# Four feature chunks of a residual turned to token rows by DMA transposes of 16-bit halves instead of TensorE transposes

## The chip, the cores and the metric

The kernel runs on one core of a Trainium2 chip. The metric is device time in microseconds of one execution, taken as the median of the runs. Engine names are those of the profile: PE is TensorE's matmul, PEld its weight load, DVE is VectorE, ACT is ScalarE, POOL is GpSimd, SP is SyncE, which issues most loads.

## The reference

One layer of a streaming encoder on 512 tokens of 1024 features, all in 32-bit floats:

```python
hn = rmsnorm(h, norm_mix_g)
proj = hn @ w_in                       # queries, keys, values, gates of two mixers
h = h + concat(forgetting_attention(...), hgrn2_recurrence(...)) @ w_out
h = h + cross_attention(rmsnorm(h, norm_x_g), rmsnorm(mem, norm_mem_g), w_xq, w_xkv, w_xo)
u = rmsnorm(h, norm_ff_g) @ w1         # 1024 -> 4096
h = h + square(relu(u)) @ w2           # 4096 -> 1024
return rmsnorm(h, final_norm_g)
```

## The kernel before

Every matrix product is made of three matmuls of numbers split in a high part (`wh...`, rounded by a ScalarE copy, line 207) and a low part (`wl...`, the rest, by a VectorE subtraction, line 212). The MLP's products follow Strassen's scheme: a group of 512 hidden units has seven block products, named 1 to 7, and weights of some of them are sums of blocks.

The change lies in the stage between cross attention and MLP. There `residual` (line 1419) makes `h + o @ w_xo` with the features on the partitions: eight chunks `c` of 128 features by 512 tokens, each a product `xw` of 24 matmuls into a bank of its own (`mm`, three banks). The weights of two neighbouring chunks form a panel (38 to 41, halves a and b). When chunk c's product is done, VectorE adds it into `hTc(c)` (`hT`, line 1450), ScalarE writes the high part of the scaled chunk (`x`, line 1452) and VectorE the low part (line 1453). Then `hooks[c]`, here `at4`, `at5` and `at6` (lines 2228 to 2249), prepare the MLP's first group: splits of its first weights, sums of its blocks (`wr`, line 1829), scaled copies of `hT` (line 1974) and their differences `xd` (line 1989), from which the operands `xs` of products 5, 6, 7 and 3 are made (lines 2003 to 2016).

The last products of the kernel want the residual with tokens on the partitions: `acc[tb]`, four tiles of 128 tokens by 1024 features. So each chunk is also turned: `tok_T` (line 1668) makes four TensorE transposes of 128x128 into a PSUM bank `ht`, `tok_copy` copies them to `acc`, half on ScalarE and half on VectorE (lines 1678 and 1680). `residual` calls this for two chunks at a time, after chunks 2, 4 and 6; chunks 6 and 7 follow inside the first group of the MLP (line 2290). `acc` is first read in the MLP's second group.

Loads stand on SP's queue, which issues them in order; each waits for the buffer it writes. The blocks of the first group are `wru01`, `wru02`, `wru05` and `wru06`: the loads of line 1810 for products 1 and 2 and for the sums. Work on each engine stands in an order that the scheduler sets from priorities; from chunk 7 on (line 2258) the order of ScalarE and VectorE is written out by hand. `behind(at, first, why)` (line 189) orders one instruction after another on its engine. `t2` tiles are 2 KB for each partition, ten buffers.

Of the kernel before, what the change touches and what calls it, by code (L numbers as in the profile page):

```python
# [9 lines left out]
F32 = mybir.dt.float32  # L10
R = mybir.dt.float32r
U8 = mybir.dt.uint8
AF = mybir.ActivationFunctionType
ALU = mybir.AluOpType
AX = mybir.AxisListType

P = 128
S = 512
NT = S // P
# [17 lines left out]
FX = (4.4, 4.4, 5.4, 5.4), (3.3, 3.9, 4.5, 5.1)  # L37
X1, X2, X3, X4 = 1.5, 2.0, 1.5, 2.0
NEG = -3.0e38
SEVEN = (1, 2, 3, 4, 5, 6, 7)  # L40
RAWS, HB, LOADS = 5, 4, 8
COPIES = {12: 2, 19: 1, 20: 0, 24: 1}
# [4 lines left out]
def emit(  # L47
# [21 lines left out]
    nc = tc.nc  # L69
    te, ve, ac, gp = nc.tensor, nc.vector, nc.scalar, nc.gpsimd  # L70
# [38 lines left out]
    def t2(name, dt=F32, shape=(S,)):  # L109
        return t2p.tile([P] + list(shape), dt, tag="t2", name=name)  # L110

    def sm(n, name):
        if n > 8:
            return s3p.tile([P, n], F32, tag="s3", name=name, padded_shape=[P, 32])
        return smp.tile([P, n], F32, tag="sm", name=name, padded_shape=[P, 8])
# [13 lines left out]
    def f(a):  # L129
        return a.bitcast(F32)  # L130
# [58 lines left out]
    def behind(at, first, why):  # L189
        tc.add_manual_dep(at.ins, first.ins.name, order_only, reason=why)  # L190
# [7 lines left out]
    def split_made(name, what, at):  # L198
        at_split[name, what] = at
        if (name, what) in pinned:  # L200
            behind(at, pinned[name, what], "split later")

    def split_of(hi, lo, raw, name=None):
        def split(what="hl"):
            at = None
            if "h" in what:
                at = ac.activation(hi, raw, AF.Copy)  # L207
                split_made(name, "h", at)
# [37 lines left out]
    def load_next(parts=(1, 1), between=None):  # L246

        i = len(stream)
        if i >= len(specs):
            return []  # L250
        if callable(specs[i]):
            return specs[i]()
        units, splits = [], []
        uk = specs[i][0][1].shape[1] // 2
        for n in range(2):
            note = None if between is None else (lambda q, at=sum(parts[:n]): between(at + q))
            unit, some = load_unit(f"{i}{'ab'[n]}", specs[i], slice(n * uk, (n + 1) * uk), parts[n], note)
            units.append(unit)
            splits += some
        stream.append(tuple([u[x] for u in units] for x in range(2)))  # L260
        return splits
# [211 lines left out]
    act0 = sm(1, "act0")  # L473
    ac.activation(act0, zero[:, 0:1], AF.Identity)
    first = load_next((4, 2), more_x)
# [24 lines left out]
    def norm_rows(t, name):  # L500
        ms = sm(2, name + "m")
        for i in range(2):
            junk = t2(f"{name}j{i}")
            ac.activation(junk, t[:, i * S : (i + 1) * S], AF.Square, scale=1.0 / 32.0, accum_out=ms[:, i : i + 1])
        ve.tensor_tensor(ms[:, 0:1], ms[:, 0:1], ms[:, 1:2], ALU.add)
# [5 lines left out]

    mku = cp.tile([P, 2, 6, 32], U8, name="mku")
    for half in range(2):
# [41 lines left out]
    def sum_jobs(kind, g):  # L555
        block = {"u": block1, "d": block2, "q": block_q}[kind]
        shape = [P, 2, S] if kind == "d" else [P, UK, WT]
        for name in SUMS:
            wsum[kind, g, name] = drp.tile(shape, F32, name=f"ws{kind}{g}{name}")

        def first(name):
            dma = nc.sync.dma_start(wsum[kind, g, name], block(g, SUMS[name][0]))
            copied.add((kind, g, name))
            return dma

        def sums():
            for name, (_, b) in SUMS.items():
                while (kind, g, name) not in copied:
                    copies.popleft()()
                src = wsum[kind, g, b] if b in SUMS else block(g, b)  # L570
                more = {"max_dma_last_dim": 2048} if b in SUMS else {}
                yield gp.dma_start(wsum[kind, g, name], src, accum_op=ALU.add, **more)  # L572

        return [lambda name=name: first(name) for name in SUMS], sums()
# [32 lines left out]
    for g in range(DFF // HG):  # L607
        if g + 1 in SEVEN:
            sets.append(sum_jobs("u", g + 1))
# [19 lines left out]
    def x_hi(c):  # L629
        ac.activation(hn_hi[:, c, :], xps[c], AF.Identity, scale=g_mix[:, c : c + 1])  # L630

# [3 lines left out]
    def x_park(c):  # L635
        part, dst = c // 2, park[:, c, :]
        if c % 2 == 0:
            ac.activation(dst, xps[c], AF.Copy)
        else:
# [5 lines left out]
    def x_sq(tb):  # L645
        junk = s4([D], f"x0j{tb}")
        if tb < 3:
            ac.activation(junk, xt[:, tb, :], AF.Square, scale=1.0 / 32.0, accum_out=ms0[:, tb : tb + 1])
        else:
# [5 lines left out]
    with tc.manual_schedule(engines={mybir.EngineType.Activation, mybir.EngineType.DVE}):  # L655
# [56 lines left out]
        for c in range(KC):  # L712
            if c in (1, 2):
                rows_of(c, wt0[0], hn_hi)
                rows_of(c, wt0[1], hn_hi)
                at = rows_of(c, wt0[0], hn_lo)
# [46 lines left out]
        def qt_(h):  # L763
            return (Mv, Sa)[h % 2][h // 2][:, h % 2, :]
# [58 lines left out]
    for hp in range(2):  # L823
# [8 lines left out]
        for j in range(2):  # L832
# [4 lines left out]
            at = ac.activation(qt_(h), qt_(h), AF.Silu)  # L837
# [111 lines left out]
    for hp in range(2):  # L949
        Ac.append(t2(f"Ac{hp}", F32, (8, 64)))  # L950
        at = ve.tensor_tensor(Ac[hp], dgs[hp], id64.unsqueeze(1).to_broadcast([P, 8, 64]), ALU.mult)
        for j in range(2):
            h = 2 * hp + j
            at = ve.tensor_tensor(qt_(h), qt_(h), Fg[hp][:, j, :], ALU.mult)
# [52 lines left out]
    for li, m in enumerate(mlev):  # L1007
# [8 lines left out]
        for hp in range(2):  # L1016
            M_ = Mv[hp]
            mix = mixed[hp]
            w = 64 if m == 64 else 32
# [8 lines left out]
        for hp, ps in enumerate(lvs):  # L1028
# [8 lines left out]
            else:  # L1037
                A_ = s4([8, P], f"A{hp}")
                Ag.append(A_)
                lo_, hi_ = slice(0, 64), slice(64, P)  # L1040
# [129 lines left out]
    for c in range(NT):  # L1170
# [27 lines left out]
        with ahead(P1):  # L1198
            hs = sm(4, f"hs{c}")
            for h in range(4):  # L1200
                j = t2(f"hj{c}{h}", F32, (P,))
                at = ac.activation(j, po[:, h, :], AF.Square, scale=128.0 ** -0.5, accum_out=hs[:, h : h + 1])
# [72 lines left out]
    def fox_bias(u):  # L1275
# [5 lines left out]
        gp.tensor_scalar(bi[:, 0:n], fF[h][:, 0:n], -1.0, Ft[:, tb, h : h + 1], op0=ALU.mult, op1=ALU.add)  # L1281
        gp.affine_select(out=bi[:, ts_], in_=bi[:, ts_], compare_op=ALU.is_ge, fill=NEG, base=0, pattern=[[-1, P]], channel_multiplier=1)

# [10 lines left out]
    def fox_softmax(u, ps):  # L1294
        p, tb, j = u
        h, n = 2 * p + j, (tb + 1) * P
        with ahead(P3):

            b = prob[u][:, 0:n]
            mx = sm(1, f"mx{h}{tb}")  # L1300
            ve.tensor_tensor_reduce(out=b, in0=ps[:, 0:n], in1=b, scale=-1.0, scalar=-NEG, op0=ALU.add, op1=ALU.min, accum_out=mx)  # L1301
            den = sm(1, f"dn{h}{tb}")
# [66 lines left out]
    for n in range(len(pairs) + 2):  # L1369
        if n < len(pairs):  # L1370
            p, tb = pairs[n]
# [41 lines left out]
    def hTc(c):  # L1413
        return hT[c // 2][:, c % 2, :]

    run_now(fill_rest(fill))
    load_hT()

    def residual(src_hi, src_lo, g, dst, name, ssq, order, nlast, after=None, hooks={}, open_end=False):

        ps_, gens = {}, {}

        def open_(c):
            if c % 2 == 0:
                open_.wt = next_panel()
            ps_[c] = mm(f"{name}{c}")
            gens[c] = gemm_fm(ps_[c], open_.wt, (c % 2) * P, src_hi, src_lo, order=order, late=True)

        def early():

            for ks in (range(UK), range(UK, KC - nlast)):
                for c in range(3):
                    if c not in gens:
                        open_(c)
                    for _ in ks:
                        yield next(gens[c])

        def rest():
            for _ in range(nlast if gens else 0):
                for gen in list(gens.values()):  # L1440
                    yield next(gen)
            for c in range(KC):
                if c not in gens:
                    open_(c)
                yield from gens[c]
                if open_end and c == KC - 1:
                    last_xw.append(ps_[c])
                    return
                hc = hTc(c)
                ve.tensor_tensor(hc, hc, ps_[c], ALU.add)  # L1450
                hi_, lo_, src = dst(c, hc)
                ac.activation(hi_, src, AF.Identity, scale=g[:, c : c + 1])
                ve.scalar_tensor_tensor(lo_, src, g[:, c : c + 1], f(hi_), op0=ALU.mult, op1=ALU.subtract)
                if ssq is None:
                    pass
                elif c == 0:
                    ac.activation(ssq, hc, AF.Square)
                else:
                    sq = t2(f"{name}sq{c}")
                    ac.activation(sq, hc, AF.Square)  # L1460
                    gp.tensor_tensor(ssq, ssq, sq, op=ALU.add)
                if after is not None and c in (2, 4, 6):
                    after(c - 2)
                    after(c - 1)
                hooks.get(c, lambda: None)()

        return early, rest
# [194 lines left out]

    acc = []

    def to_tok(c):
        tok_copy(c, tok_T(c))

    def tok_T(c):
        ps = tr(f"ht{c}")
        for tb in range(NT):  # L1670
            te.transpose(ps[:, tb * P : (tb + 1) * P], hTc(c)[:, tb * P : (tb + 1) * P], ident)
        return ps

    def tok_copy(c, ps):
        for tb in range(NT):
            d, s_ = acc[tb][:, c * P : (c + 1) * P], ps[:, tb * P : (tb + 1) * P]
            if tb % 2 == 0 or c > 5:
                ac.activation(d, s_, AF.Copy)
            else:
                ve.tensor_copy(d, s_)  # L1680
# [577 lines left out]
    with tc.manual_schedule(engines={mybir.EngineType.Activation, mybir.EngineType.DVE}):  # L2258
        c = KC - 1
# [109 lines left out]
```

## Time and profile before

| | |
|---|---|
| median of 3 runs | 737.67 us (737.52 to 737.95) |
| the profiled execution | 737.33 us, span 735.6 us |
| PE busy | 728.3 us, 99% |
| DVE busy | 596.8 us, 81% |
| ACT busy | 489.2 us, 67% |
| POOL busy | 177.5 us, 24% |
| DMA | 163.89 MB, 223 GB/s in the mean |
| granted TensorE clock | 0.999 |

A row of the timeline gives start and duration in us, engine, line, operation, output and input, and in brackets the idle time of the engine before it and who ended it. A row of the chain gives start, duration, engine, name and line. The profile names tiles without their numbers: `wru` is any of the blocks above, `ht` any of the transposed chunks. A shape is partitions by elements.

The stage in stretches that begin and end at chunk borders of TensorE's stream, with the busy time of each engine (count of instructions in brackets):

```profile
389.30:395.60 6.30, 6.30 (x33) 5.37 (x32) 6.22 (x11) 5.39 (x11) 0.82 (x2) 1.00 0.81 164
395.60:401.10 5.50, 5.50 (x25) 4.48 (x25) 2.90 (x6) 1.67 (x2) 1.53 (x2) 1.00 1.06 273
401.10:407.40 6.30, 6.30 (x33) 5.38 (x32) 4.16 (x8) 3.78 (x8) 1.56 (x2) 1.00 0.93 184
407.40:412.90 5.50, 5.50 (x26) 4.48 (x25) 4.83 (x5) 1.67 (x2) 0.94 (x1) 1.00 0.62 98
412.90:419.20 6.30, 6.30 (x33) 5.36 (x32) 5.25 (x10) 4.25 (x9) 1.12 (x2) 1.00 0.77 94
```

The columns are the stretch and its length, then PE, PEld, DVE, ACT and POOL busy, the granted clock, the mean busy share of the DMA engines, and GB/s.

### The profile page before, as it was taken

To read this page: it belongs to the slowest core of one execution; us is meant where nothing else is said; L and a number is where in the kernel's file an instruction comes from. 1 tells how busy PE (TensorE), PEld (TensorE's weight loads), DVE (VectorE), ACT (ScalarE), POOL (GpSimd) and SP (SyncE) were. 2 spreads that over 40 slices of the span, in tenths; PEclk is the share of its full clock that TensorE was granted. 3 is DMA by queue.
4 is the path that set the end of the run, shared out by engine and by line. 5 is a ranking of instruction groups with operands and counts; after the bars stand their busy time and mean duration, and the time that the engine had idled before them with its cause. 6 is when DMAs were issued, how large, how long until landed. Compare 5 with 4: busy or idle time off the path is not lost.

```text
span 735.6 us, 11788 instructions
## 1 busy us (share of the span) xinstructions
PE 728.3 (99%) x4227; PEld 625.1 (85%) x4227; DVE 596.8 (81%) x1006; ACT 489.2 (67%) x850; POOL 177.5 (24%) x253
## 2 busy tenths in 40 slices
PE   9999999999999999999999999999999999999996
PEld 6789888998888888889988898888888888888885
DVE  6868997777877846767747898998989898989896
ACT  5967776566666644547535589777676767684964
POOL 7122101443432415422111202111111111100024
PEclk9999999999999999999999999999999999999999
DMA  7789969847946999987868799989998899978352
GB/s 244 240 235 257 329 217 294 279 172 239 340 165 195 289 297 267 226 186 145 210 130 185 119 243 230 248 233 258 211 263 210 242 243 229 249 190 249 121 115 114
DMA packets 115819, 163.89 MB, mean 223 GB/s; under 512 B 6529, under 2 KB 77482, under 8 KB 115762
## 3 DMA queue, kind: packets, MB, share of 16 engines
q1 hardware_dynamic: 87538, 117.24, 47.6%
q0 software_dynamic: 28064, 45.64, 34.8%
q8 instruction: 33, 0.54, 0.3%
q10 hardware_dynamic: 160, 0.27, 0.1%
q14 instruction: 24, 0.20, 0.1%
HBM read 157.87 MB, written 54.54 MB: 289 GB/s over the span
## 4 chain that ended last, share of the span: by engine, by line
PE 97%; issue 1%; DMA 1%; DVE 0%; ACT 0%; POOL 0%; POOLq 0%; DVEq 0%
PE uU L1939 11%; PE uY L1939 5%; PE U L2097 4%; PE U L2098 4%; PE U L2099 4%; PE uV L1939 3%; PE xk L1260 2%; PE wo L373 2%; PE xw L373 2%; PE xw L374 2%; PE xw L375 2%; PE wo L375 2%; PE wo L374 2%; PE Y L2099 2%; PE Y L2098 2%; PE Y L2097 2%
## 5 line engine op out<-in xcount | busy, mean ns | idle before, releaser
L207 ACT ACTIVATE whu<-wru 128x1024 fp32r<-128x1024 f32 x53 | 55.1, 1059 | 36.6 <-PE U L2099 17.7
L212 DVE TENSOR_TENSOR wlu<-wru,whu 128x1024 fp32r<-128x1024 f32 x53 | 64.1, 1220 | 12.0 <-ACT whu L207 12.0
L212 DVE TENSOR_TENSOR wld<-wrd,whd 128x1024 fp32r<-128x1024 f32 x56 | 67.9, 1216 | 1.7 <-ACT whd L207 1.7
L207 ACT ACTIVATE whd<-wrd 128x1024 fp32r<-128x1024 f32 x56 | 59.3, 1060 | 10.5 <-PE uU L1939 2.9
L2097 PE MATMUL U<-whd,hb 128*128 128x512 f32 x120 | 46.8, 390 | 0.0
L2098 PE MATMUL U<-wld,hb 128*128 128x512 f32 x120 | 46.8, 390 | 0.0
L2099 PE MATMUL U<-whd,hb 128*128 128x512 f32 x120 | 46.7, 389 | 0.0
L1281 POOL TENSOR_SCALAR bi<-nF,Ft 128x128 f32<-128x128 f32 (+3 forms) x32 | 20.2, 639 | 53.1 <-PE pt L1326 37.0
L572 POOL DMA_DIRECT2D wsd<-in_w_dram x16 | 17.5, 1094 | 59.1 <-PE xw L375 13.7
L1786 POOL DMA_DIRECT2D wrd<-in_w_dram x8 | 9.8, 1222 | 88.1 <-DVE wld L212 76.9
L1786 POOL DMA_DIRECT2D wru<-in_w_dram x7 | 9.2, 1315 | 79.6 <-DVE wlu L212 79.6
L1939 PE MATMUL uY<-xs,whu 128*128 128x512 f32 x112 | 28.0, 392 | 0.0
L1939 PE MATMUL uU<-x,whu 128*128 128x512 f32 x112 | 27.7, 389 | 0.0
L1939 PE MATMUL uU<-xs,whu 128*128 128x512 f32 x112 | 27.7, 389 | 0.0
L2064 DVE SCALAR_TENSOR_TENSOR acc<-Y,acc 128x512 f32<-128x512 f32 x28 | 19.0, 685 | 10.2 <-PE Y L2099 9.8
L2099 PEld LDWEIGHTS U<-whd,hb 128*128 128x128 f32 x120 | 22.5, 188 | 4.7
L2097 PEld LDWEIGHTS U<-whd,hb 128*128 128x128 f32 x120 | 22.6, 188 | 4.5
L2098 PEld LDWEIGHTS U<-wld,hb 128*128 128x128 f32 x120 | 22.6, 188 | 4.4
L572 POOL DMA_DIRECT2D wsu<-in_w_dram x14 | 17.8, 1271 | 34.8 <-PE xw L375 17.7
L1303 ACT ACTIVATE bi<-bi,mx 128x128 f32<-128x128 f32 (+3 forms) x32 | 17.9, 560 | 11.2 <-DVE mx L1301 10.0
L2097 PE MATMUL Y<-whd,hb 128*128 128x512 f32 x64 | 24.9, 389 | 0.0
L2098 PE MATMUL Y<-wld,hb 128*128 128x512 f32 x64 | 24.9, 389 | 0.0
(1061 smaller groups left out, 2546.9 us busy)
## 6 DMA issues: line engine op xcount, KB each, us to landing
wru<-in_w_dram SPq DMA_DIRECT2D x25, 512.0 KB, 6.9
wsd<-in_w_dram SPq DMA_DIRECT2D x24, 512.0 KB, 7.5
wrd<-in_w_dram SPq DMA_DIRECT2D x24, 512.0 KB, 7.0
wrd<-wsd SPq DMA_DIRECT2D x24, 512.0 KB, 6.0
wsu<-in_w_dram SPq DMA_DIRECT2D x21, 512.0 KB, 8.6
wru<-wsu SPq DMA_DIRECT2D x21, 512.0 KB, 5.8
wsd<-in_w_dram POOLq DMA_DIRECT2D x16, 512.0 KB, 8.2
wsu<-in_w_dram POOLq DMA_DIRECT2D x14, 512.0 KB, 9.2
```

The source lines that it names most:

```text
L207: at = ac.activation(hi, raw, AF.Copy)
L212: at_lo = ve.tensor_tensor(lo, raw, f(hi), ALU.subtract)
L373: te.matmul(ps, wh, hi, start=n_ == 0 and not begun, stop=False)
L374: te.matmul(ps, wb, lo, start=False, stop=False)
L375: at = te.matmul(ps, wc, hc, start=False, stop=k == order[-1])
L572: yield gp.dma_start(wsum[kind, g, name], src, accum_op=ALU.add, **more)
L1281: gp.tensor_scalar(bi[:, 0:n], fF[h][:, 0:n], -1.0, Ft[:, tb, h : h + 1], op0=ALU.mult, op1=ALU.add)
L1786: tc.keep_in_program_order(gp.dma_start(box[0], block(g, "10"), accum_op=ALU.add))
L1939: at = te.matmul(out_, w[:, k, ws], x_[:, k, :], start=begin, stop=end, skip_group_check=True)
L2097: te.matmul(ps, hi, whi[:, k, :], start=begin, stop=False, skip_group_check=True)
L2098: te.matmul(ps, hi, wlo[:, k, :], start=False, stop=False, skip_group_check=True)
L2099: at = te.matmul(ps, lo, whi[:, k, :], start=False, stop=k == 1, skip_group_check=True)
```

## The change

Chunks 0 to 3 leave TensorE. A chunk's 32-bit words are seen as pairs of 16-bit halves. ScalarE copies the chunk apart, first all lower halves and then all upper ones (`hw`, 128 x 2 x 512). A DMA on SP's queue that transposes 16-bit elements turns the eight blocks of 128x128 halves into `tw` (token on the partition; half, token block, feature along the row). Copies on ScalarE and VectorE then put the halves together again as 32-bit words in `acc`. Chunks 0 and 1 are put into `acc` after chunk 5, chunks 2 and 3 after chunk 6; chunks 4 and 5 keep the TensorE transposes and also follow after chunk 6. Chunks 6 and 7 are as before.

```diff
+U16 = mybir.dt.uint16
+XB = 4
+AT = {5: (0, 1), 6: (2, 3, 4, 5)}
...
                 hi_, lo_, src = dst(c, hc)
-                ac.activation(hi_, src, AF.Identity, scale=g[:, c : c + 1])
-                ve.scalar_tensor_tensor(lo_, src, g[:, c : c + 1], f(hi_), op0=ALU.mult, op1=ALU.subtract)
+                at_parts[:] = (
+                    ac.activation(hi_, src, AF.Identity, scale=g[:, c : c + 1]),
+                    ve.scalar_tensor_tensor(lo_, src, g[:, c : c + 1], f(hi_), op0=ALU.mult, op1=ALU.subtract),
+                )
...
-                if after is not None and c in (2, 4, 6):
-                    after(c - 2)
-                    after(c - 1)
+                if after is not None:
+                    to_halves(c)
+                    for c_ in AT.get(c, ()):
+                        after(c_)
                 hooks.get(c, lambda: None)()
...
+    halves = {}
+
+    def words(ap):
+        return ap.bitcast(U16).rearrange("p (n w) -> p w n", w=2)
+
+    def to_halves(c):
+        if c < XB:
+            own, turned = t2(f"hw{c}", U16, (2, S)), t2(f"tw{c}", U16, (2, NT, P))
+            ac.activation(own, words(hTc(c)), AF.Copy)
+            nc.sync.dma_start(turned.rearrange("p w t n -> p (w t) n"), own.rearrange("p w n -> p (w n)"), transpose=True)
+            halves[c] = turned
+
     def to_tok(c):
-        tok_copy(c, tok_T(c))
+        if c not in halves:
+            return tok_copy(c, tok_T(c))
+        turned = halves.pop(c)
+        for tb in range(NT):
+            d, s_ = words(acc[tb][:, c * P : (c + 1) * P]), turned[:, :, tb, :]
+            at = ac.activation(d, s_, AF.Copy) if tb % 2 == 0 else ve.tensor_copy(d, s_)
+            behind(at, at_parts[tb % 2], "parts first")
```

Three queues change their order. In the rows below the number behind a name tells buffers apart, and line numbers of the changed kernel are a few higher.

SP's queue, the loads of the first group (`wru`) before:

```order
L235 DMA wr41b_4529<-in_w_xo_dram 128x4x256
L1810 DMA wru01_4582<-in_w1_dram 128x4x256
L1810 DMA wru05_4586<-in_w1_dram 128x4x256
L1810 DMA wru06_4588<-in_w1_dram 128x4x256
L1810 DMA wru02_4584<-in_w1_dram 128x4x256
L1768 DMA wru11_4746<-in_w1_dram 128x4x256
```

and now:

```order
L238 DMA wr41b_4527<-in_w_xo_dram 128x4x256
L1836 DMA wru05_4566<-in_w1_dram 128x4x256
L1836 DMA wru06_4568<-in_w1_dram 128x4x256
L1836 DMA wru01_4562<-in_w1_dram 128x4x256
L1682 DMA_TRANSPOSE tw0_4471<-hw0_4470 128x8x128
L1682 DMA_TRANSPOSE tw1_4478<-hw1_4477 128x8x128
L1682 DMA_TRANSPOSE tw2_4485<-hw2_4484 128x8x128
L1682 DMA_TRANSPOSE tw3_4518<-hw3_4517 128x8x128
L1836 DMA wru02_4564<-in_w1_dram 128x4x256
L1794 DMA wru11_4742<-in_w1_dram 128x4x256
```

The two blocks for the sums moved ahead of `wru01`, and the four transposing transfers stand between `wru01` and `wru02`.

ScalarE, from the split of panel 40b to that of panel 41b, before:

```order
L207 ACTIVATE wh40b_4346<-wr40b_4348 128x1024
L1452 ACTIVATE x2_0_4164<-hT0_3275,gv_245 128x2x256 x2
L1452 ACTIVATE x2_0_4164<-hT1_3277,gv_245 128x2x256
L1678 ACTIVATE acc0_4444<-ht0_4476 128x128
L1678 ACTIVATE acc0_4444<-ht1_4485 128x128
L1974 ACTIVATE hT0_3275<-hT0_3275,gv_245 128x512 x2
L207 ACTIVATE wh41a_4523<-wr41a_4525 128x1024
L1678 ACTIVATE acc2_4446<-ht0_4476 128x128
L1678 ACTIVATE acc2_4446<-ht1_4485 128x128
L207 ACTIVATE wh41b_4527<-wr41b_4529 128x1024
```

and now:

```order
L210 ACTIVATE wh40b_4346<-wr40b_4348 128x1024
L1458 ACTIVATE x2_0_4164<-hT0_3275,gv_245 128x2x256
L1681 ACTIVATE hw0_4470<-hT0_3275 128x1024
L1458 ACTIVATE x2_0_4164<-hT0_3275,gv_245 128x2x256
L1458 ACTIVATE x2_0_4164<-hT1_3277,gv_245 128x2x256
L210 ACTIVATE wh41a_4521<-wr41a_4523 128x1024
L1681 ACTIVATE hw1_4477<-hT0_3275 128x1024
L2000 ACTIVATE hT0_3275<-hT0_3275,gv_245 128x512
L1681 ACTIVATE hw2_4484<-hT1_3277 128x1024
L1458 ACTIVATE x2_0_4164<-hT1_3277,gv_245 128x2x256
L1681 ACTIVATE hw3_4517<-hT1_3277 128x1024
L210 ACTIVATE wh41b_4525<-wr41b_4527 128x1024
```

All four `hw` copies and the high part of chunk 3 now stand ahead of the split of panel 41b, and the small copies from `ht` are gone.

VectorE, from the low part of chunk 5 to the split for product 5, before:

```order
L1453 SCALAR_TENSOR_TENSOR x2_1_4165<-hT2_3279,gv_245,x2_1_4165 128x2x256
L1829 TENSOR_TENSOR wr05_4634<-wru01_4582,wru05_4586 128x1024
L1829 TENSOR_TENSOR wr06_4636<-wr05_4634,wru06_4588 128x1024
L1450 TENSOR_TENSOR hT3_3281<-hT3_3281,xw6_4638 128x512
L1680 COPY acc1_4445<-ht4_4667 128x128
L1453 SCALAR_TENSOR_TENSOR x2_1_4165<-hT3_3281,gv_245,x2_1_4165 128x2x256
L1680 COPY acc3_4447<-ht4_4667 128x128
L1680 COPY acc1_4445<-ht5_4676 128x128
L1989 TENSOR_TENSOR xd5_4692<-hT2_3279,hT0_3275 128x512
```

and now, from the same place:

```order
L1459 SCALAR_TENSOR_TENSOR x2_1_4165<-hT2_3279,gv_245,x2_1_4165 128x2x256
L1691 COPY acc1_4445<-tw0_4471 128x2x128
L1691 COPY acc3_4447<-tw0_4471 128x2x128
L1691 COPY acc1_4445<-tw1_4478 128x2x128
L1691 COPY acc3_4447<-tw1_4478 128x2x128
L1855 TENSOR_TENSOR wr05_4622<-wru01_4562,wru05_4566 128x1024
L1855 TENSOR_TENSOR wr06_4624<-wr05_4622,wru06_4568 128x1024
L1455 TENSOR_TENSOR hT3_3281<-hT3_3281,xw6_4626 128x512
L1706 COPY acc1_4445<-ht4_4663 128x128
L1706 COPY acc1_4445<-ht5_4672 128x128
L1459 SCALAR_TENSOR_TENSOR x2_1_4165<-hT3_3281,gv_245,x2_1_4165 128x2x256
L1691 COPY acc1_4445<-tw2_4485 128x2x128
```

Four copies from `tw` now stand ahead of the two sums, and four more (the first is shown) behind the low part of chunk 6. On TensorE the only difference is that the transposes of chunks 0 to 3 are gone.

More of the change, by code (lines that the diff above doesn't have):

```diff
@@ L1417, in emit @@
     load_hT()
+    at_parts = []
     def residual(src_hi, src_lo, g, dst, name, ssq, order, nlast, after=None, hooks={}, open_end=False):
```

## The prediction

> **What bounds the kernel now.** I read the page first (shares of the engines, chain of work), then what TensorE waited for, then the timeline of the stage that the change touches, engine by engine.
>
> ```profile
> span 735.6 us, 11788 instructions
> PE 728.3 (99%) x4227; PEld 625.1 (85%) x4227; DVE 596.8 (81%) x1006; ACT 489.2 (67%) x850; POOL 177.5 (24%) x253
> PE 97%; issue 1%; DMA 1%; DVE 0%; ACT 0%; POOL 0%; POOLq 0%; DVEq 0%
> ```
>
> The chain that ended last runs through TensorE for 97% of the span. The view of waits, restricted to TensorE, has two rows, both from the start of the program:
>
> ```profile
> PE warm L487 <- PEq L2355: 0.8, 1, 0.8
> PE gf L669 <- ACT hn_hi L630: 0.3, 1, 0.3
> ```
>
> So TensorE waits for nobody near the change or after it. What is taken out of its stream comes off the end, as long as nobody else gets late. The program is one execution of 737.33 us with a span of 735.6 (1.7 us lie outside the span); the median of the runs, 737.67, is 0.34 above it, and I add my difference to the median.
>
> **What is removed from TensorE.** The chain of work, in order of time, where the two groups of eight transposes (chunks 0 and 1, then 2 and 3) stand:
>
> ```profile
> 389.46 0.88 PE ht L1671 x8
> ...
> 401.26 0.87 PE ht L1671 x8
> ```
>
> Eight transposes hold the chain for 0.88 and 0.87 us, 0.11 each. The third group (chunks 4, 5) and the fourth (6, 7) stay. Removed: 0.88 + 0.87 = **1.75 us**, all of it on the path. No more than this can be won here.
>
> **What is added on ScalarE and VectorE.** The evictions of the removed transposes go: eight copies of 128x128 on each engine.
>
> ```profile
> L1678 ACT ACTIVATE acc<-ht x20: 251/277/353, 391.6 to 433.5; 128x128 f32<-128x128 f32 x20
> L1680 DVE COPY acc<-ht x12: 282/285/291, 393.2 to 416.8; 128x128 f32<-128x128 f32 x12
> ```
>
> (line, engine, operation, count: shortest/middle/longest in ns.) In their place come eight copies of 256 halves on each. No row shows a 16-bit copy with a stride; by element count the nearest rows are these, 0.37 us on ScalarE (mean ns after the bar) and 0.42 on VectorE:
>
> ```profile
> L1922 ACT ACTIVATE sq<-uU 128x256 f32<-128x256 f32 x14 | 5.0, 371 | 0.0
> ```
> ```profile
> L1989 DVE TENSOR_TENSOR xd<-xg,hT x2: 418/418/419, 421.7 to 422.0; 128x256 f32<-128x256 f32 x2
> ```
>
> Bounds: 0.28 (the same bytes as an old copy) and twice the row. I take 0.37 and 0.42, since cost follows the element count in these rows; instructions that follow each other overlap by some 0.09 (two copies of 0.285 below take 0.48), so each fills about 0.33 us of VectorE where an old copy filled 0.2. ScalarE also gets four copies of 1024 halves (`hw`); nearest row is a 128x1024 split:
>
> ```profile
> 389.78 1.93 ACT L1452 ACTIVATE x<-hT,gv 128x512 fp32r<-128x512 f32 x3
> ...
> 395.86 1.06 ACT L207 ACTIVATE wh41b<-wr41b 128x1024 fp32r<-128x1024 f32 x1 [1.17 <-PE xw L375]
> ...
> 401.74 0.28 ACT L1678 ACTIVATE acc<-ht 128x128 f32<-128x128 f32 x1 [4.21 <-PE ht L1671]
> ...
> 407.63 1.06 ACT L207 ACTIVATE whu<-wru 128x1024 fp32r<-128x1024 f32 x1 [1.66 <-PE xw L375]
> ```
>
> That is about 0.97 each back to back, 3.9 in all (between 0.5 each, for half the bytes, and 2 each). ScalarE has room: 4.21 us of idle before 401.74 cover it. But all four now stand ahead of the split `wh41b`. That split starts at 395.86 before; it gets 3.9 (four `hw`) and 0.6 (the high part of chunk 3, also moved ahead) more before it, and loses four small copies (0.8), one scaling (0.6) and its idle 1.17: it starts about 1.9 later, near 397.8. The product that reads panel 41b starts at 410.15 (row further down), 8 us after the split's low part even then, so nothing waits there. One effect remains: the wrp buffer of panel 41b, which the load of block `wru02` waits for, comes free 1.9 later.
>
> VectorE is the engine with little room:
>
> ```profile
> 396.95 1.23 DVE L212 TENSOR_TENSOR wl41b<-wr41b,wh41b 128x1024 fp32r<-128x1024 f32 x1 [0.33 <-ACT wh41b L207]
> ...
> 410.53 1.22 DVE L1829 TENSOR_TENSOR wr<-wru,wru 128x1024 f32<-128x1024 f32 x1
> 411.78 1.22 DVE L1829 TENSOR_TENSOR wr<-wr,wru 128x1024 f32<-128x1024 f32 x1
> 413.07 0.69 DVE L1450 TENSOR_TENSOR hT<-hT,xw 128x512 f32<-128x512 f32 x1
> 413.82 0.29 DVE L1680 COPY acc<-ht 128x128 f32<-128x128 f32 x1
> 415.04 0.75 DVE L1453 SCALAR_TENSOR_TENSOR x<-hT,gv,x 128x512 fp32r<-128x512 f32 x1 [0.93 <-ACT x L1452]
> 415.71 0.48 DVE L1680 COPY acc<-ht 128x128 f32<-128x128 f32 x2
> ...
> 419.42 0.69 DVE L2263 TENSOR_TENSOR hT<-hT,xw 128x512 f32<-128x512 f32 x1
> ...
> 423.11 1.23 DVE L2016 TENSOR_TENSOR xs<-xd,xs 128x1024 fp32r<-128x1024 f32 x1
> ```
>
> Between 410.53 and 413.76 it has no gap, and from 413.07 to 419.42 one gap of 0.93. Eight copies of 0.33 fall into this stretch, four ahead of the sum at 410.53 and four after the residual add at 413.07, where TensorE meanwhile arrives 1.75 earlier. Following the order: the first four push the add of chunk 6 about 1.0 behind TensorE (1.3 minus small gaps); the second four (1.3) fill the gap of 0.93 and add a few tenths; the small copies and the two moved `xd` pieces give some back. The add of chunk 7, at 419.42 before, is then about 1.0 late against TensorE. What it holds up:
>
> ```profile
> 410.15 0.39 PE L373 MATMUL xw<-o_hi,wh41b 128*128 128x512 f32 x1
> ...
> 424.25 0.28 PE L1887 MATMUL uV<-x,whu 128*128 128x256 f32 x1
> ...
> 424.97 0.28 PE L1887 MATMUL uY<-xs,whu 128*128 128x256 f32 x1
> ```
>
> Product 2 reads chunk 7 at 424.25; its low part is done 1.2 us ahead of that (it ends where the row at 423.11 begins). Product 5 reads the low part that the row at 423.11 makes, done at 424.34 against 424.97: 0.63 of slack. With VectorE 1.0 late, product 2 just holds and product 5 waits about 0.2 to 0.4. I take **0.2**; the ends are 0 (copies as cheap as the old ones) and 2.8 (each copy fills 0.66, 2.6 us more in all).
>
> **The transposing transfers and SP's queue.** Four transfers now stand on SP's queue between the loads of `wru01` and `wru02`. What is queued behind them: `wru02`, then the loads of the next group. Nobody but the accumulator copies waits for the transfers themselves, 12 us or more after the `hw` copy. `wru02` is the term. The issue (count and ns, first and last start), POOL's (q0) and SP's (q1) queue in the window from 391 to 404 us (packets, MB, share of 16 engines), and the landing of such loads between 370 and 440 us:
>
> ```profile
> L1810 SPq DMA_DIRECT2D wru<-in_w_dram x4: 368/434/499, 391.4 to 398.2; - x4
> ```
> ```profile
> q0 software_dynamic: 621, 1.11, 54.9%
> q1 hardware_dynamic: 2081, 2.07, 47.9%
> ```
> ```profile
> wru<-in_w_dram SPq DMA_DIRECT2D x7, 512.0 KB, 5.1
> ```
>
> `wru02` was issued last of the four, at 398.2, when `wl41b` ended. Its split on ScalarE ran at 407.63, held by TensorE alone (the weight buffer), so now 405.9. Changed: its buffer is free at 398.2 + 1.9 = 400.1; issue 0.4 and landing 5.1 (the median of seven such loads) give 405.6, which is 0.3 in time. Two other loads, `wru05` and `wru06`, go ahead of `wru01` and wait only for TensorE, so they leave the busy stretch. ScalarE's order from 389.78 (0.62 for each high part or scaling, 0.97 for a split) lets the four `hw` copies end near 391.5, 394.7, 396.2 and 397.8; with a price of t per transfer the queue is through at the latest of 391.8 + 4t and 394.7 + 3t. Up to t = 1.8 that is before 400.1 and costs nothing. Above it, each further us of t makes `wru02` 3 to 4 us later, its split holds up VectorE in order, and the gain is gone at about t = 2.5.
>
> No row shows t. A plain issue holds SP for 0.37. By bytes: SP's queue moved 2.07 MB in 47.9% of 13 us, 3.0 us per MB, so 0.26 MB take **0.8**. By packets: 2081 of them in those 6.2 us, 3.0 ns each; a transfer is 1024 rows of 128 halves (256 bytes), so 3.1. I take 1.0, nearer to the bytes, because a packet of that queue carries 1 KB and one of these a quarter.
>
> The Trainium skill, "Advanced Engine Details and Errata", section X-Bar Transpose (TRN2), calls such transfers as fast as ordinary ones, 350 to 400 GB/s; an estimate from that is 0.7 us each, and the sum would be the same as mine. "VectorE: DVE Perf Modes", section The three transpose paths, says the opposite: 1309 ns for a 128x128 block against 390 ns on TensorE; its rules for kernel authors advise TensorE where PSUM will do. For TensorE the trace disagrees (0.11 us each in a row of eight). For the transfer no row decides; an estimate from that page, eight blocks, is 10.5 us for each transfer, and by it the time would be some 769 us.
>
> **The sum.** 737.67 - 1.75 + 0.2 = **736.1**. After this stage TensorE has no wait, and the loads there are released by buffers that TensorE frees, so the shift stays.
>
> **Rivals.**
> - **The queue is late, moderately** (t from 2 to 4). For: the packet bound is 3.1, and the two queues' shares, 54.9 and 47.9%, add up to full DMA engines. Against: two loads of 512 KB leave this stretch. At 3.1 the queue is through at 391.8 + 12.4 = 404.2, `wru02` has landed at 409.7 and its split, with all of VectorE behind it, is 3.8 late. Of product 2's slack of 1.2 VectorE's own 1.0 leaves 0.2, so TensorE waits 3.6, and 0.2 in product 5: 737.67 - 1.75 + 3.8 = 739.7. It decides from t = 2.5, where the split is 1.75 late.
> - **The transfers are dear** (t above 4). Then everything on ScalarE and VectorE behind the split of `wru02` shifts by 4 us for each us of t: at t = 4 the queue is through at 407.8, the split 7.4 late, the time 743.3; at t = 6 it is 751. For: blocks of 16-bit halves are a kind of transfer that no row shows. Against: a price above even the packet bound. The block price of "VectorE: DVE Perf Modes" in the Trainium skill, told above, would lie here.
> - **VectorE eats the gain** with the transfers cheap: strided 16-bit copies that fill 0.45 to 0.66 instead of 0.33 make the wait 1.2 to 2.8: 737.1 to 738.7, no change. For: VectorE's one gap there is 0.93. Against: no row has a copy that costs more than its elements.
>
> **Chances.** Likeliest case 0.50 (735.9 to 736.6); late queue 0.22; dear transfers 0.18; VectorE 0.10. About 0.2% (1.5 us) is what a measurement of this kernel can tell from no change, and the forecast gain of 1.55 is hardly more. Faster: 0.75 of the likeliest case and a little of the late queue and VectorE, 0.41. Same: the rest of the likeliest, a third of the late queue, most of VectorE, 0.27. Slower: the rest, 0.32. The range goes from 735.6 (the whole 1.75 won, and 0.3 for the spread of runs) to 744 (t = 4), which leaves out most of the dear transfers. The likeliest case's own range is 735.7 to 736.7.
>
> **What the profile after should show.** Two groups of `ht` instead of four on the chain; TensorE's `xw` products starting 0.88 and then 1.75 earlier; a wait of 0.2 to 0.4 at product 5 (`uY`) on VectorE's `xs`. SP's four transposing transfers issued near 391.8, 394.7, 396.3 and 397.9, and `wru02` near 400. Wrong: a wait of ScalarE's `whu` on the DMA of `wru02`, or of the accumulator copies on `tw`; a wait of TensorE on `x` in product 2; copies from `tw` above 0.45 us on VectorE.

## The result, and the profile after

The changed kernel takes 755.02 us (751.76 to 760.35) against 737.6 for the kernel before on the same chip: a ratio of 1.024, 95% interval 1.021 to 1.027. It is 17.4 us slower; the forecast was 736.1, with 744 as its upper end. The profiled execution took 754.54 us. Its page begins with these lines (span, TensorE, the chain that ended last):

```profile
span 752.8 us, 11767 instructions
PE 731.2 (97%) x4211; PEld 627.3 (83%) x4211; DVE 595.9 (79%) x1006; ACT 494.7 (66%) x854; POOL 178.4 (24%) x253
PE 91%; DMA 3%; DVE 2%; SPq 2%; ACT 1%; issue 1%; POOL 0%; POOLq 0%; DVEq 0%; ACTq 0%
```

TensorE has 16 matmuls fewer, as foreseen, and the chain of work now goes through a DMA and through SP's queue. The view of TensorE's waits (who waited for whom: us in total, times, longest) has three rows that were not there before, all at the second product of the MLP's first group:

```profile
PE uV L1913 <- DVE hT L1455: 10.9, 1, 10.9
PE uV L1913 <- ACT x L2292: 3.4, 1, 3.4
PE uV L1914 <- DVE x L2296: 0.7, 1, 0.7
```

That is 15.0 us. The timeline of SP's queue shows what is late (start, time on the queue, line, operation, tile, count):

```profile
391.82 0.37 SPq L1836 DMA_DIRECT2D wru<-in_w_dram  x1
392.28 16.69 SPq L1682 DMA_TRANSPOSE tw<-hw  x4
409.07 0.53 SPq L1836 DMA_DIRECT2D wru<-in_w_dram  x1
```

The four transposing transfers hold the queue for 16.69 us, 4.2 each, and the load of `wru02` behind them is issued at 409.07 (before: 398.2). (1.2 us of the stretch is a wait of the second transfer for its `hw` copy; the four issues alone add up to 15.2. Prices per transfer below are such stretches divided by the number of transfers.) The view of the tile `tw` gives the issues (shortest, middle, longest in ns) and the landing, which the trace has for three of the four:

```profile
L1682 SPq DMA_TRANSPOSE tw<-hw x4: 1581/2655/8320, 392.3 to 400.7; - x4
DMA to landing us min/median/max: 11.4/15.7/18.9
```

The load itself then takes very long. Rows of the chain, of ScalarE's and of VectorE's timeline:

```profile
409.07 15.70 DMA wru<-in_w_dram
```
```profile
424.86 1.06 ACT L210 ACTIVATE whu<-wru 128x1024 fp32r<-128x1024 f32 x1 [20.23 <-DMA wru<-in_w_dram]
```
```profile
425.95 1.23 DVE L215 TENSOR_TENSOR wlu<-wru,whu 128x1024 fp32r<-128x1024 f32 x1 [18.97 <-ACT whu L210]
```

ScalarE stands 20.23 us in front of the split of `wru02`, VectorE 18.97, and behind them in order stands the add of chunk 6, for which TensorE waits 10.9 us. A second loss shows in no row of waits. The table by stretches (stretch, length, PE, PEld, DVE, ACT, POOL busy, granted clock, DMA share, GB/s):

```profile
392.00:418.60 26.60, 26.60 (x125) 22.19 (x125) 10.23 (x13) 10.76 (x14) 5.31 (x5) 1.00 1.30 145
418.60:431.80 13.20, 2.33 (x21) 2.16 (x19) 5.82 (x11) 4.07 (x10) 0.89 (x1) 0.66 0.72 141
431.80:440.00 8.20, 4.56 (x19) 4.06 (x19) 7.81 (x17) 7.51 (x15) 0.00 (x0) 0.71 0.14 44
440.00:445.00 5.00, 4.58 (x27) 4.58 (x28) 4.83 (x8) 4.41 (x7) 0.00 (x0) 0.66 0.40 130
445.00:470.00 25.00, 25.00 (x177) 23.49 (x177) 21.97 (x28) 22.80 (x43) 4.98 (x6) 1.00 0.87 223
```

While and after TensorE waits, the granted clock is 0.66 to 0.71 instead of 1.00. By an estimate from these rows (busy time by one less the clock), PE's 2.33, 4.56 and 4.58 us of work there would have been 0.8, 1.3 and 1.6 shorter at full clock: 3.7 us. (PE is busy 731.2 us here and 726.5 with as many matmuls in the held-back version below.) The account of the span: 15.0 of waits + 3.7 of clock - 1.75 of transposes = 17.0; measured 752.8 - 735.6 = 17.2.

### The profile page after: what moved, and what is told of

Read it like the earlier page. It is cut to its first block, busy times and chain, and to the rows that moved or that the text cites. A ratio compares the mean times of both kernels' runs of the same rounds, so it can differ in the third digit from the quotient of the medians.

```text
span 752.8 us, 11767 instructions
## 1 busy us (share of the span) xinstructions
PE 731.2 (97%) x4211; PEld 627.3 (83%) x4211; DVE 595.9 (79%) x1006; ACT 494.7 (66%) x854; POOL 178.4 (24%) x253
## 4 chain that ended last, share of the span: by engine, by line
PE 91%; DMA 3%; DVE 2%; SPq 2%; ACT 1%; issue 1%; POOL 0%; POOLq 0%; DVEq 0%; ACTq 0%
PE uU L1965 10%; PE uY L1965 5%; PE U L2123 4%; PE U L2124 4%; PE U L2125 4%; PE uV L1965 3%; DMA wru<-in_w_dram 2%; PE xk L1263 2%; PE wo L376 2%; PE wo L378 2%; PE wo L377 2%; PE Y L2124 2%; PE Y L2123 2%; PE Y L2125 2%; SPq L1682 2%; PE pv L1347 1%
## 5 line engine op out<-in xcount | busy, mean ns | idle before, releaser
L575 POOL DMA_DIRECT2D wsd<-in_w_dram x16 | 17.5, 1094 | 76.0 <-PE uY L1915 23.7
```

## The experiments

Why did four transfers of 256 KB cost so much? Theories: **A**, transposing transfers are dear by themselves; **B**, only SP's queue behind them counts; **C**, they are dear because of what runs beside them. At 395.0, 400.0 and 404.5 POOL starts three of its pre-sums (line 575, a job list that follows TensorE's progress): transfers of 512 KB that add a weight block onto another in DRAM (`accum_op`), for later groups; below they are called accumulating. In the texts of expectation, theory Q is B, theory D is a form of A (many small packets fill the DMA engines), and V puts the loss on the copies of ScalarE and VectorE; their "product 2", "6" and "7" are the products `xw` of those chunks. The ratio in brackets is always to the kernel before, run beside, with its 95% interval.

**Plain copies in place of transposing ones.**

```diff
-nc.sync.dma_start(turned..., own..., transpose=True)
+nc.sync.dma_start(turned..., own...)
```

> The changed kernel with the four transfers from hw to tw as plain copies of the same 256 KB (rows of 2 KB) and not transposed, so the first four chunks reach acc unturned; order of all engines unchanged. Theory D (the transposing itself fills the DMA engines with 4096 small packets) and theory Q (each transposing transfer holds SP's queue for 2 to 8 us, so the load of wru02 goes out at 409 and not at 400): the plain transfers cost SP 0.4 us each, wru02 is issued near 400 and lands near 406; no wait of TensorE, 735.9 to 736.7 us. Theory V (the copies hw and tw on ScalarE and VectorE are what is late): the wait of TensorE on chunk 6 stays, above 745 us.

Measured: 739.95 us (1.0035, 1.002 to 1.005). About 15 us go away with the transposing, but the kernel is still no faster than before. ScalarE's timeline, the tile `tw` and TensorE's waits:

```profile
409.06 1.06 ACT L210 ACTIVATE whu<-wru 128x1024 fp32r<-128x1024 f32 x1 [5.11 <-PE xw L378]
```
```profile
DMA to landing us min/median/max: 7.1/7.6/8.0
```
```profile
PE uV L1913 <- ACT x L2292: 1.1, 1, 1.1
PE uV L1914 <- DVE x L2296: 0.7, 1, 0.7
PE uY L1914 <- DVE xs L2042: 0.3, 1, 0.3
```

`wru02` was issued at 399.71, where I had put it (400.1). Its split could start only at 409.06, 9.35 us later; the row names TensorE, but in the held-back version below the same split starts at 405.91, held by TensorE, so what came last here was most likely this load (the trace has no landing for it). I had given it 5.1 us. So two terms were wrong: the price of a transposing transfer, and the landing of a load among the others.

**The load of `wru02` from ScalarE's queue**, past the four transfers (theory B against A and C).

```diff
-first_dma.append(nc.sync.dma_start(raw, block1(0, rc)))
+first_dma.append((nc.scalar if rc == "10" else nc.sync).dma_start(raw, block1(0, rc)))
```

> The changed kernel with the load of wru02 issued from ScalarE's queue (behind the scaling of chunk 3), everything else as it is. Theory Q: it is issued near 401, lands near 406 to 407, its split runs near 407; TensorE waits 0 to 1 us, 736 to 738 us. Theory D: it is issued near 401 but shares the DMA engines with the transposing packets, lands at 412 or later (11 us or more instead of 5), TensorE waits 5 us or more, 743 to 750 us.

Measured: 750.36 us (1.019, 1.015 to 1.022). ScalarE's timeline:

```profile
399.98 0.42 ACTq L1836 DMA_DIRECT2D wru<-in_w_dram  x1
...
418.80 1.06 ACT L210 ACTIVATE whu<-wru 128x1024 fp32r<-128x1024 f32 x1 [14.58 <-DMA wru<-in_w_dram]
```

Issued 9 us earlier, it is split only 6 us earlier: 18.8 us from issue to split. Theory B explains about 5 us of 17; the load itself is slow, whichever queue it is in.

**Two chunks in place of four** (`XB = 2`).

> Only chunks 0 and 1 by transposing transfers (put into acc after chunk 5), chunks 2 and 3 by TensorE after chunk 4 as in the kernel before; TensorE's stream is 0.88 us shorter than before. Both theories: the queue is through near 397 to 399, before the buffer of wru02 is free near 399. Theory Q: wru02 lands near 405, no wait, 736.6 to 736.9 us. Theory D: 2048 packets of 60 ns are 7.7 us of all 16 engines beside POOL's transfers, so wru02 and the blocks for the sums behind it land 2 to 5 us late (wru02 near 407 to 410), TensorE waits 1 to 4 us, 738 to 741 us.

Measured: 740.93 us (1.005, 1.003 to 1.006). The two transfers hold SP for 5.03 us, 2.5 each: the price is not a constant of the transfer, and half of them cost a fifth of the loss. (In this version the two loads for the sums stand behind them again; they landed 17.0 and 17.5 us after issue.)

**The transfers by themselves**, in a kernel of their own.

> The transfers by themselves; the layer is left out. In order: one transposing transfer of 128x1024 halves with nothing else on the DMA engines, four of them in a row, one plain copy of the same 256 KB, four of these, one transposing transfer of a single 128x128 block, and four transposing transfers beside four loads of 512 KB issued by POOL. Theory D: one transposing transfer takes the 16 engines about 3.8 us (1024 packets at 60 ns), four in a row about 15, a plain one below 1 us; SP is held only while the engines' queues are full. Theory Q: the engines are done with one in about 1 us and SP is held 2 to 4 us for each, also in a row on empty engines.

SP's timeline has, first, four transposing transfers with nothing beside them, and then four beside four loads of 512 KB from POOL's queue:

```profile
11.42 5.36 SPq L25 DMA_TRANSPOSE tb<-s  x4
...
27.02 13.33 SPq L25 DMA_TRANSPOSE tg<-s  x4
```

Alone they hold SP 1.34 us each and land 1.1 to 1.5 us apart, beside POOL's loads 3.3 each. The 1.0 that I took was near the price alone. This speaks against A and for C.

**POOL's three transfers held back** from the end of chunk 2 to the product of chunk 6, all else as in the changed kernel.

```diff
-while self.jobs and self.spent >= self.next:
+while self.jobs and self.spent >= self.next and not self.hold:
...
+if after is not None:
+    presum.hold = 2 <= c < 5
```

> The changed kernel, with POOL's accumulating transfers of the pre-summed weights held back from the end of product 2 until the start of product 6 (the three that started at 395.0, 400.0 and 404.5 start after 407 instead); nothing else moved. Theory C (the transposing transfers are dear only beside POOL's transfers): each takes the 1.1 to 1.5 us that four in a row took alone, SP is held about 5 to 6 us instead of 16.7, wru02 is issued near 400 instead of 409.1 and lands by 406 to 409, the wait of 10.9 in front of the next stage goes, and the kernel takes 736 to 740 us. Rival A (the transfers are dear by themselves at this place, whatever runs beside them): SP is held more than 12 us, wru02 is issued after 405, and the kernel takes over 748 us.

Measured: **735.35 us** (0.997, 0.996 to 0.998), 20 us less than the changed kernel and 2.15 less than the kernel before. The page, SP's timeline and POOL's:

```profile
PE 726.5 (99%) x4211; PEld 623.6 (85%) x4211; DVE 595.8 (81%) x1006; ACT 494.2 (67%) x854; POOL 178.1 (24%) x253
```
```profile
391.90 9.09 SPq L1685 DMA_TRANSPOSE tw<-hw  x4
401.09 0.53 SPq L1839 DMA_DIRECT2D wru<-in_w_dram  x1
```
```profile
406.85 1.04 POOL L575 DMA_DIRECT2D wsd<-in_w_dram  x1 [16.79 <-PE xw L378]
407.85 1.23 POOL L575 DMA_DIRECT2D wsu<-in_w_dram  x1
408.48 1.67 POOL L575 DMA_DIRECT2D wsd<-in_w_dram  x1
```

The split of `wru02`:

```profile
405.91 1.06 ACT L210 ACTIVATE whu<-wru 128x1024 fp32r<-128x1024 f32 x1 [1.66 <-PE xw L378]
```

The transfers now hold SP 2.3 us each, `wru02` goes out at 401.09, and its split starts at 405.91, held by TensorE alone. TensorE has no wait in this stage, and is busy 1.8 us less than before. Theory C holds in direction, not in size: 5 to 6 us on the queue and 736 to 740 us were expected, 9.09 and 735.35 came. An earlier accumulating transfer, not held back, was in flight until 395.05, and the load of `wru01` was issued just ahead; which of them keeps the price above 1.34 was not tested. The same three transfers held back in the **kernel before**, as a control:

> The kernel before, with only POOL's three accumulating transfers held back until product 6, and TensorE's transposes kept. If holding them back is a gain of its own (theory: less contention for the loads), this kernel too comes to 735.4 to 736.5 us, and the transposing transfers had no part in the gain of the held-back version. If the gain there is that of the removed transposes (theory C), this one stays at 737.2 to 737.8 us.

Measured: 737.50 us (1.000, 0.999 to 1.001). Holding back is worth nothing by itself; the gain is that of the transposes.

**Chunks 0 to 3 not turned at all**, in the kernel before (`if after is not None and c == 6:`, and zeros in `acc`).

> The kernel before, with chunks 0 to 3 of the residual not brought to token rows at all (that part of the output accumulator is filled with zeros by POOL at the start of the stage; 16 TensorE transposes and their 16 copies are left out, and no transfer takes their place). It bounds from above what the change can bring. If TensorE's own work is the limit there, the two groups of eight transposes, 0.88 and 0.87 us, go: 1.75 us less, 735.7 us. If the loads or ScalarE and VectorE set the end as soon as TensorE has less to do, less than 1 us goes: 736.5 to 737.5 us.

Measured: 735.73 us (0.998, 0.997 to 0.999), PE busy 726.5. The 1.75 us were right, and the held-back version has all that there is to win here (it stands 0.4 lower still, within the two intervals).

**`wru02` loaded early** into a buffer that is free sooner, ahead of the transfers; POOL's transfers as in the changed kernel.

```diff
+if rc == "10":
+    raw = k4([UK, WT], f"wr{name}")
-if rc[1] == "0":
+elif rc[1] == "0":
     raw = wrp.tile(...)
```

> The changed kernel, with wru02 loaded into another buffer that is free sooner, so that it is issued ahead of the four transposing transfers and before 390; POOL's transfers stay where they were. If the late load of wru02 is the only way in which the transfers cost anything (theory: SP queue and landing of that load), all of the 15 us goes and the kernel takes 736 to 738 us. If the transposing transfers still land 11 to 19 us after issue, the copies of what they deliver are waited for next: ScalarE and VectorE stand in front of product 7's add until the third and fourth have landed, near 415 to 420, TensorE waits 4 to 10 us, and the kernel takes 741 to 747 us.

Measured: 742.68 us (1.007, 1.005 to 1.010). ScalarE's timeline and TensorE's largest wait:

```profile
418.52 0.84 ACT L1691 ACTIVATE acc<-tw 128x256 uint16<-128x256 uint16 x2 [4.58 <-DMA tw<-hw]
```
```profile
PE uV L1915 <- ACT x L2294: 2.4, 1, 2.4
```

With the load out of the way, the copies out of `tw` wait for the transfers, and the next group waits for them (3.4 us of TensorE's waits in all; 4 to 10 were expected). Some 12 of the 17 us had gone by way of `wru02`, the rest by way of the copies; both come from the same transfers.

**Both edits together.**

> The changed kernel with both edits: wru02 loaded early into the other buffer, and POOL's transfers held back until product 6. Theory C with the price alone (1.1 to 1.5 us for each transfer, landing within 10 us): nothing is late any more, the 1.75 us of transposes are gained, less up to 1 us for copies and start-up: 735.5 to 737 us, a little faster than before. If the transfers stay dear (rival A): over 741 us, as with the early load alone. If the transfers of POOL, three at once after 407, make the first loads of the next stage late: 738 to 742 us.

Measured: 735.49 us (0.997, 0.996 to 0.998). The early load adds nothing once the transfers are quick.

**Small plain pieces.** What about the transfers is it that suffers: the 256-byte pieces, or the transposing?

```diff
-nc.sync.dma_start(turned..., own..., transpose=True)
+nc.sync.dma_start(turned..., own[:, 1, 0:P].unsqueeze(1).to_broadcast([P, 2 * NT, P]))
```

> The changed kernel with plain copies in place of the transposing transfers, but in 1024 pieces of 256 bytes each, as many as a transposing transfer has (the first high-half block is written eight times, so chunks 0 to 3 of that part of the output are not the reference's). Theory C1 (what is dear beside POOL's transfers is the number of small packets, one turn each): SP is held over 10 us, the transfers land 10 us and more after issue, wru02 is issued after 405 and the kernel takes 745 to 755 us, as the changed one. Theory C2 (it is the transposing itself, which small plain packets don't share): SP is held under 4 us, wru02 is issued by 401 and the kernel takes 738 to 741 us, as with the plain copies in large pieces (739.95).

Measured: 743.36 us (1.008, 1.007 to 1.010), between the two theories. The tile `tw`:

```profile
DMA to landing us min/median/max: 8.0/8.6/10.8
```

Small pieces cost 3.4 us more than large ones (739.95); transposing adds 11.7 to that. The Trainium skill ("DMA: Bandwidth & Descriptors", section Queues, rings and completion order) says that a DMA engine takes turns between its queues packet by packet. No run here shows the turns. If a queue of small packets loses to one of large ones for that reason, the 3.4 us would fit; the 11.7 need something else.

**Beside plain loads**, with no layer around it.

> The layer is left out; the kernel only moves data, in six phases: four transposing transfers of 256 KB alone, twice; four of them beside four loads of 512 KB issued from ScalarE's queue; four beside four such loads issued from POOL's queue; then four plain transfers in pieces of 256 bytes beside loads from ScalarE's queue, and beside loads from POOL's queue. Theory C as the held-back version shows it: 1.3 us each alone; beside the loads from ScalarE's queue 2 to 2.5 us each (all four landed within 10 us); beside those from POOL's queue 3.5 us and more each (13 to 16 us for the four, as the 15.3 before); the plain small pieces under 2.5 us each beside either. Rival (any load of that size stretches them, whichever queue issues it): the third and fourth phase take the same 13 to 16 us. Second rival (small pieces suffice, transposing or not): the last phase takes as long as the fourth.

The phases ran into each other (the loads from ScalarE's queue began while the second phase's last transfer was under way), so the third and fifth phase decide nothing. Nearly clean are the fourth and the sixth: transposing (`td`) and small plain pieces (`tf`), each beside four plain loads of POOL (loads from ScalarE's queue run into the last 2.4 us of the fourth, and the fifth's last transfer lands 1.2 us into the sixth).

```profile
L25 SPq DMA_TRANSPOSE td<-sc x4: 1308/2919/4406, 33.8 to 44.2; - x4
...
DMA to landing us min/median/max: 3.5/8.2/10.8
```
```profile
L41 SPq DMA_DIRECT2D tf<-se x4: 594/2419/4397, 58.3 to 64.1; - x4
...
DMA to landing us min/median/max: 8.0/9.9/11.7
```

They landed 13.9 and 13.8 us after the first issue: the second rival was right here. In this one execution, beside plain loads, transposing has no price beyond its small pieces. In the kernel it has one. One thing that differs there is that POOL's transfers accumulate.

**POOL's three transfers without the addition**: at the same place, of the same size, as plain copies.

```diff
-yield gp.dma_start(wsum[kind, g, name], src, accum_op=ALU.add, **more)
+add = {} if 276 < presum.next < 287 else {"accum_op": ALU.add}
+yield gp.dma_start(wsum[kind, g, name], src, **add, **more)
```

> The changed kernel, with the three POOL transfers that start at 395.0, 400.0 and 404.5 made plain copies in place of accumulating ones (three of the pre-sums then lack their first operand); everything else, the transposing transfers too, as in the changed kernel. If it is the accumulating that stretches the transposing packets: SP is held under 10 us for the four, as when POOL's transfers are held back (9.1), wru02 is issued by 402, and the kernel takes 736 to 743 us. If any large transfer of POOL's queue does it: SP is held 13 us and more, wru02 is issued after 405, and the kernel takes 748 to 757 us.

Measured: 736.86 us (0.999, 0.998 to 1.000), 18 us less than the changed kernel; the queue and the issue of `wru02` are a little later than expected (10 us, 402). SP's timeline:

```profile
392.64 10.69 SPq L1683 DMA_TRANSPOSE tw<-hw  x4
403.43 0.53 SPq L1837 DMA_DIRECT2D wru<-in_w_dram  x1
```

The DMA view of both kernels between 402 and 409 us (packets, MB, share of 16 engines; q0 is POOL's queue, q1 SP's), first the changed kernel, then the one without the addition:

```profile
q1 hardware_dynamic: 1383, 0.34, 90.3%
q0 software_dynamic: 302, 0.39, 58.9%
```
```profile
q1 hardware_dynamic: 2744, 1.07, 58.4%
q0 software_dynamic: 288, 1.05, 37.6%
```

With the addition a packet of SP's queue lasted 73 ns on its engine (0.903 x 7 us x 16 / 1383), without it 24 ns, and the core moved 0.73 MB instead of 2.12. (Most packets are small in both: under 512 bytes 1399 of 1685, and 2264 of 3032. This window shows the difference at its largest; between 393 and 401 us the same working gives 50 and 40 ns.) POOL's three transfers suffer too: they land 11.6, 14.5 and 12.9 us after issue in the changed kernel, 8.4, 8.3 and 6.2 in the kernel before. That is the cause of most of the loss: transposing transfers and accumulating ones in flight together slow each other and the loads beside them. Why they do so, no run here shows; whether it is the addition itself or other traffic that comes with it was not separated.

**Six chunks by transfers**, held back and with the early load (`XB = 6`).

> Held back and wru02 loaded early, with six chunks by transfers in place of four (24 TensorE transposes of 32 gone), POOL's transfers held until the end of product 6. If the price of a transfer stays near 2.3 us and its copies come late enough, a third group of eight transposes (0.87 us) goes too: 734.3 to 735.2 us. If the fifth and sixth transfer, issued near 403 and 408, land after their copies stand at the head of ScalarE's and VectorE's queues, product 7's add waits for them: 737 to 742 us.

Measured: 738.35 us (1.001, 1.000 to 1.002). No wait for `tw` or `x` appears; TensorE has small waits of 0.3 to 0.6 us for splits and operands of the next groups, 2.0 us in all. The time lies in the second expected range, but not by its cause. It is 2.9 above the four-chunk version (735.49), where 0.87 less was hoped for; the waits explain 2.0 of these 3.7 us, and the rest is open.

## Why the prediction was wrong, point by point

- **The 1.75 us removed**: right. PE busy falls by 1.8 wherever the transfers don't disturb.
- **ScalarE's copies**: right in the main. `hw` took 1.04, 0.95 back to back (0.97 taken), the copies out of `tw` 0.47 (0.37 taken; four in a row fill 1.48), and `wh41b` was split at 398.07 (397.8 foreseen).
- **VectorE's copies**, 0.2 us: too much. A run of four fills 0.91, 0.23 each (0.33 taken); the wait at product 5 does not appear in the held-back version, only (0.3 us) in versions where ScalarE and VectorE are late. That rival had nothing to it.
- **The price t of a transposing transfer**: the step that failed. I took 1.0, between 0.8 by bytes and 3.1 by packets; it was 4.2. Alone it is 1.34, with POOL's three transfers held back 2.3, beside plain transfers of POOL 2.7 to 3.3, beside accumulating ones 4.2. What ran beside the transfers had no place in the price. My upper bound took each transposing packet as no dearer than the packets of that window, 3.0 ns of 16 engines; with 73 ns on one engine it was 4.6. Both bounds came from other kinds of packets, and I called a value "above even the packet bound" unlikely for no better reason. That nobody would have to wait for the transfers themselves failed with it: they landed up to 18.9 us after issue, and in the early-load version ScalarE waits 4.58 us for them.
- **The landing of `wru02`**, 5.1: the second term that failed. The row's "x7, 5.1" counts seven loads, but its median is over those whose landing the trace has. Read in narrower windows, the view gives a landing for one alone, issued at 419.34, behind this stage; for the four loads of the stage it has none. So 5.1 was never a measurement of this place. The load took at most 9.35 us (issue to split) with plain copies in place of the transfers, and 15.7 in the changed kernel.
- **The rival "the transfers are dear"** had the mechanism and the chain right: SP's queue, the split of `wru02`, VectorE behind it in order, then TensorE. The first sign of being wrong that the prediction names, a wait of ScalarE's `whu` on the DMA of `wru02`, is the row of 20.23 us. Its own rule gives 743.3 for a split 7.4 late, and one us for each further one; at 18.97 late that is 754.9, against 755.02 measured. That the two agree so closely is luck: the rule leaves out the 3.7 us of clock, and TensorE's waits were 4 us shorter than the split was late. It is the chain that is shown, not the figure. The rival's price was too small, and its chance, 0.18, too low. The break-even (t = 2.5; the prediction's own terms give 2.6) fits roughly: at 2.3 the kernel wins 2.15 us, at 2.7, without the addition, 0.6.
- **The pages of the Trainium skill**: the estimate by "Advanced Engine Details and Errata", section X-Bar Transpose (TRN2), 0.7 us, is half of what a transfer took alone and a sixth of what it took here. The estimate by "VectorE: DVE Perf Modes", section The three transpose paths, 10.5 us, is seen in no run: eight blocks took 1.34 in a row.

## What to carry to other kernels

Before moving work to the DMA engines, list what else is in flight in those microseconds and of which kind: here a transfer cost 1.3 us alone, 2.3 with most accumulating transfers held back and 4.2 beside them, and keeping the accumulating ones out of 15 us turned 2.4% slower into 0.3% faster. When a transfer is put on an in-order queue, give the load behind it the landing time of that crowded stretch, and look at how many landings a median is made of. An unknown price whose bounds come from other kinds of transfers has no upper bound; forecast from the point where it decides, not from its middle.

## What the runs showed of the hardware

- Transposing transfers of 256 KB (four of them: 4224 packets, 1.05 MB) land 1.1 to 1.5 us apart in a row with nothing beside them. With accumulating transfers of POOL in flight, the whole core moved 0.73 MB in 7 us, with the DMA engines busy for most of it; with plain transfers in their place, 2.12 MB.
- The granted TensorE clock fell to 0.66 to 0.71 during and after a wait of 11 us, and was back at 1.00 by 445, some 13 us after that wait. In the version with two smaller waits after 418 (3.7 and 0.5 us, small plain pieces) it was 0.64 between 424 and 432. By the estimate above, the waits of TensorE in the changed kernel cost about a quarter more than their own length; no run tests the clock apart from the waits.
